# Rows of the normalised activations 2080 bytes apart instead of 2048, in one feed-forward and one convolution

## The chip, the cores and the metric

The kernel runs on one core of a Trainium2 chip, as one program. The metric is the device time of one execution in microseconds. A profile shows five engines: TensorE (PE for matmuls, PEld for loading the stationary operand), VectorE (DVE), ScalarE (ACT), GpSimd (POOL) and SyncE (SP), which issues the DMAs.

## The reference

A decoder trunk of two layers over 256 tokens of width 2048, all in float32. Layer 0 mixes tokens by multi-scale retention, layer 1 by a short gated convolution; each mixer is followed by a SwiGLU feed-forward of width 5632. Cut to the stages that the change touches:

```
h = rms_norm(x, norm2_g[0]) * (1 + sc2) + sh2          # layer 0's feed-forward
a, b = split(h @ ffn_w_in[0], 2);  x = x + g2 * ((silu(a) * b) @ ffn_w_out[0])

h = rms_norm(x, norm1_g[1]) * (1 + sc1) + sh1          # layer 1's convolution
b_gate, c_gate, u = split(h @ conv_w_in, 3)
u = c_gate * u;  y = sum(conv_w[j] * shifted(u, j) for j in range(3))
x = x + g1 * ((b_gate * y) @ conv_w_out)
```

The modulation (sc, sh, g) comes from the conditioning vector c through w_mod.

## The kernel before

**Numbers in two parts.** The width of 2048 is cut into 16 blocks of 128, one block to the 128 partitions. A float32 operand is used as two parts in a shorter format (float32r): high, the rounded value, and low, the rest. A product is then three partial products: high x high, high x low and low x high. Weights arrive by DMA as 1 MB tiles named raw; ScalarE casts 1024 columns to the high part, tile hi (L420), VectorE subtracts to get the low part, tile lo (L423). hi and lo are two fixed rings of five places of 1024 columns, and a cast waits until TensorE has read what stood in its place.

**h.** The normalised and modulated activations are one tile, h_all, of 17 x 514 columns in a partition. It holds, at different times, two layouts:

- raw rows: 16 rows, 514 columns apart: two end columns (the shift, high and low), 256 columns of scaled x (high), 256 columns (low). L642 and L643 write the 512 as x becomes ready, L654 and L655 the end columns of all rows. The first group of matmuls of a stage (L668 to L670) reads them while the norm is still being computed.
- rows of h: 16 rows of 512 columns, 256 high and 256 low. L611 (ScalarE) writes the high half, L612 (VectorE) the low half, each in the place of raw rows that have been read.

```
P, S, KT, ENDS, EARLIER = 128, 256, 16, 2, 120
h_all = hpool.tile([P, (KT + 1) * (ENDS + 2 * S)], F32R, tag="h", name="h")
```

In the retention and both feed-forwards the rows of h begin at column EARLIER of h_all, in the convolution at column 0.

**Two forms of product.** In the form by columns (`product`) the weights are stationary and h streams past: for each row k and block of 128 columns, one matmul with hi and 512 columns of h (L473), one with lo and h's 256 high columns (L476). All of the convolution's input and the first groups of each feed-forward have this form. In the form by token (`by_token`, `thrice`) 128 tokens of a row of h are stationary and 512 columns of hi or lo stream past, three matmuls for one product:

```
nc.tensor.matmul(o, hi, w_hi, start=first, stop=False)    # L486: high part of h, tile hi
nc.tensor.matmul(o, hi, w_lo, start=False, stop=False)    # L487: high part of h, tile lo
nc.tensor.matmul(o, lo, w_hi, start=False, stop=last)     # L488: low part of h, tile hi
```

Every matmul is preceded by its own load of the stationary operand (LDWEIGHTS), which runs while the matmul before it streams.

**The feed-forward's input.** It is made in column groups of 2 x 512. Each group runs over eight pairs of rows of h. Five are plain: for each of the two rows two column halves, two token halves and three matmuls, 12 per row. The other three (pairs 2, 4 and 6) use a scheme with seven products instead of eight (`sevens`), of which each is again a triple L486 to L488; the stationary operands are, in this order, s4, a12, s1, s3, a11, s2, a22. Here a11, s3 stand in the even row of the pair (s3 has replaced a part of it), a12 and a22 in the odd row, and s1, s2, s4 are sums of them in tiles of their own. Layer 0's feed-forward has four groups in its first part and six in its second. The same scheme serves in the last feed-forward's output, where mid takes h's place and the sums lie in in_cb, sums_of_tokens and other tiles.

**Order.** TensorE's order is the order in which the code is written; the other engines' is set by a scheduler, which weighs when an operand is ready. Pads such as `beside_in_sums` or `aside` hold no data; they set where the tiles behind them begin.

Of the kernel before, what the change touches and what calls it, by code (L numbers as in the profile page):

```python
# [19 lines left out]
S = 256  # L20
KT = D // P
# [22 lines left out]
ONE_GROUP = (1, 1)  # L44
FFN_TILES, FFN_SEVEN, FFN_TURNS = (20, 24), (2, 4, 6), 2
STORE_AT, LOAD_AT = 0, 2
BESIDE_IN_SUMS = 120
LEAD_RET, LEAD_CONV, LEAD_FFN = 6, 4, 2
AHEAD = 2
MOD_LEAD = 64  # L50
# [7 lines left out]
LEFT, ENDS, EARLIER = 8, 2, 120  # L58
# [207 lines left out]
def trunk(ctx: ExitStack, tc: tile.TileContext, x_in, c_in, pos_in, w_mod, cols_in, gain_in, tab_in, w_all, out):  # L266
# [12 lines left out]
    def tmp(tag, shape=(P, S), dtype=F32, pool=work, bufs=None):  # L279
        return pool.tile(list(shape), dtype, tag=tag, name=name(tag), bufs=bufs)  # L280
# [12 lines left out]
    at = [0]  # L293
# [332 lines left out]
    h_all = hpool.tile([P, (KT + 1) * (ENDS + 2 * S)], F32R, tag="h", name="h")  # L626
    hpool.tile([P, 88], F32, tag="beside", name="beside")

    def rows_at(o):
        return [  # L630
            h_all[:, o + 2 * S * j : o + 2 * S * (j + 1)].rearrange("p (a b) -> p a b", a=2) for j in range(KT)
        ]

    h = rows_at(EARLIER)
    raw_all = h_all.rearrange("p (k n) -> p k n", k=KT + 1)[:, :KT, :]

    def scaled_only(layer, norm, j):

        needed(layer, SC2 if norm else SC1, j)
        a = mod_a[layer][norm][:, j : j + 1]  # L640
        high, low = raw_all[:, j, ENDS : ENDS + S], raw_all[:, j, ENDS + S :]
        nc.scalar.activation(high, x[j], AF.Identity, scale=a)  # L642
        nc.vector.scalar_tensor_tensor(low, x[j], a, high.bitcast(F32), op0=ALU.mult, op1=ALU.subtract)  # L643
# [50 lines left out]
    def output(groups, act, which, last, after=None, base=None):  # L694

        layer, gate = which[0], mod_g[which[0]][which[1] == GT2]
        first, *groups = groups
        base, acc = first.ks[0] if base is None else base, None
        held_ks = first.ks[8 :: len(first.ks)]
        banks = product(  # L700
            first, act, base, last=False, before=lambda k: waiting.pop(0)() if waiting and k in held_ks else None
        )
        for j, g in enumerate(groups):
            needed(*which, j)
            col = gate[:, j : j + 1]
            if last and j == KT - 1:
                (pt,) = packed(g, act, base)
                nc.vector.scalar_tensor_tensor(x[j], pt[:, 0, :], col, x[j], op0=ALU.mult, op1=ALU.add)
                acc = [acc, squares(None, x[j], "acc1")]
                if after:  # L710
                    after(j)
                return acc
            (pt,) = product(g, act, base, banks=banks[j : j + 1])
            t = tmp("sum", bufs=4)
            nc.vector.scalar_tensor_tensor(t, pt[:, 1, :], col, x[j], op0=ALU.mult, op1=ALU.add)
            nc.vector.scalar_tensor_tensor(x[j], pt[:, 0, :], col, t, op0=ALU.mult, op1=ALU.add)
            if last:
                acc = squares(acc, x[j])
            if after:
                after(j)  # L720


    with ExitStack() as inner:
# [64 lines left out]
        with tc.tile_pool(name="start", bufs=1) as sp:  # L788
# [169 lines left out]
            at, plain_rows = 0.0, range(PLAIN - FIRST_KS)  # L958
# [186 lines left out]
        for n, head in enumerate(HEAD_ORDER):  # L1145
            projections(head)
            if n == HEADS // 2 - 1:
                ret_out(0, False)
        acc = ret_out(1, True)
        h = rows_at(0)  # L1150

    def sums(g):
# [38 lines left out]
    def made_in_sums(rows, single_sums):  # L1191

        for i in rows:
            both = half_bank().rearrange("p (a b) -> p a b", a=2)
            for n in range(2):
                k = 2 * i + n
                high, low = [h[k].bitcast(F32)[:, v, :] for v in range(2)]
                nc.vector.tensor_tensor(both[:, n, :], high, low, op=ALU.add)
            own["sums"][i] = [single_sums.pop() for _ in range(3)]
            tokens_sums_of(*parts(both), h[2 * i][:, :, P:], own["sums"][i])  # L1200
# [72 lines left out]
    def last_input(groups, pairs, seven):  # L1273

        ours, extra = gathered(groups, h, 0, own["sums"])
        for (t, j), pt in ours.items():
            nc.vector.tensor_tensor(extra[t, j], pt, extra[t, j], op=ALU.add)
        ms = []
        for t in range(2):
            m = extra[t, 0]  # L1280
            nc.scalar.activation(m, m, AF.Silu)
            nc.vector.tensor_tensor(m, m, extra[t, 1], op=ALU.mult)
            ms.append(m)

        def turned():
            for n, (dst, of) in enumerate(zip(pairs, seven)):
                pt = bank()
                for i in range(2):
                    for t, m in enumerate(ms):
                        c = slice((2 * n + i) * P, (2 * n + i + 1) * P)  # L1290
                        nc.tensor.transpose(pt[:, i, t * P : (t + 1) * P], m[:, c], ident)  # L1291
                if of is not None:
                    both = half_bank().rearrange("p (a b) -> p a b", a=2)
                    nc.scalar.copy(both, pt)
                nc.scalar.copy(dst[:, :, 0, :], pt)
                nc.vector.tensor_tensor(dst[:, :, 1, :], pt, dst[:, :, 0, :].bitcast(F32), op=ALU.subtract)
                if of is not None:
                    tokens_sums_of(*parts(both), of[3] if len(of) > 3 else dst[:, 0, :, P:], of[:3])

        waiting.append(turned)  # L1300

    def first_rows(firsts, pairs, layer, norm, turns=()):

        pending, done = [], 0
        for i, g in enumerate(firsts):
            pending += [sums(g)] if i else normed(acc, layer, norm, g)
            while len(pending) >= 2:
                both = half_bank().rearrange("p (a b) -> p a b", a=2)
                g1, m = both[:, 0, :], both[:, 1, :]
                silu_times(*pending[:2], g1, m)  # L1310
                pending = pending[2:]
                split(pairs[done // 2][:, done % 2], m)
                done += 1
            for turn_of in turns[4 * (i - 1) : 4 * i] if i else ():
                turn_of()

    def paired(pool, n):

        return [pool.tile([P, 2, 2, S], F32R, tag=f"mid{i}", name=name("mid")) for i in range(n // 2)]

    with tc.tile_pool(name="ffn", bufs=1) as fpool:
        h = rows_at(EARLIER)
        own.update(pool=fpool, sums={}, turns=FFN_TURNS)
        first_mid = paired(fpool, max(FFN_TILES))[: FFN_TILES[0] // 2]
        differences[0] = fpool.tile([P, 2 * DV], F32, tag="differences", name="differences")
        own["extra"] = [fpool.tile([P, DV], F32, tag=f"extra{i}", name=f"extra{i}") for i in range(2)]
        for part in range(2):
            n = FFN_TILES[part] // 2
            mid = paired(fpool, FFN_TILES[part]) if part else first_mid
            if not part:  # L1330
                first_rows(FFN_FIRSTS, mid[-2:], 0, 1)
                fpool.tile([P, BESIDE_IN_SUMS], F32, tag="beside_sums", name="beside_in_sums")
                made_in_sums(FFN_SEVEN, [
                    fpool.tile([P, 2, P], F32R, tag=f"sums{i}", name=f"sums{i}") for i in range(6)
                ] + [tmp("u", (P, 2, P), F32R, bufs=3) for _ in range(3)])
            for i, groups in enumerate(FFN_IN[part]):
                last_input(groups, mid[2 * i : 2 * i + 2], [None, None])
            act = {k + part * FFN_TILES[0]: mid[k // 2][:, k % 2] for k in range(2 * n)}
            acc = output(
                FFN_OUT[part], act, (0, GT2), part == 1, (lambda j: scaled_only(1, 0, j)) if part else None, base=0  # L1340
            )
        h = rows_at(0)

    mixing = ctx.enter_context(ExitStack())
    mpool = mixing.enter_context(tc.tile_pool(name="mpool", bufs=1))
# [3 lines left out]
    for i, g in enumerate(CONV_IN):  # L1349
        pending += [sums(g)] if i else normed(acc, 1, 0, g)  # L1350
        while len(pending) >= 3:
            pb, pc, pu = pending[:3]
            pending = pending[3:]
            j = done
            b, c, u = pb(tmp("bsum", pool=mpool, bufs=2)), pc(), pu()
# [20 lines left out]
    h = rows_at(EARLIER)  # L1376
# [187 lines left out]
```

## Time and profile before

| what | value |
|---|---|
| runs | 2564.65, 2557.89, 2558.99 us; median 2558.99 |
| profiled execution | 2558.53 us, its span 2556.8 us |
| TensorE busy | 2539.5 us, 99% of the span, granted clock 0.999 |
| VectorE, ScalarE, GpSimd busy | 92%, 53%, 7% |
| read from HBM | 685.11 MB, mean 269 GB/s |

Some rows of the profile are groups: line, engine, operation, output<-inputs, shapes, count; then busy time in us and the mean ns of one; then the idle time before them. Others are the timeline: start in us from the span's start, duration in us, engine, line, operation and, in brackets, idle time before it with what ended it. TensorE's matmuls are pipelined, so a row's duration is longer than the distance to the next row's start; the pace is read from the starts, which the timeline gives to 10 ns.

### The profile page before, as it was taken

The numbers are of one execution on the slowest core, as the hardware profiler recorded it, in microseconds if no ns is written. First come the engines' busy times: TensorE is split into PE (matmuls) and PEld (weight loads), VectorE is DVE, ScalarE is ACT, GpSimd is POOL, SyncE is SP. The second block draws the span as 40 slices with busy tenths as digits, with TensorE's granted clock in tenths as the row PEclk, the third lists the DMA queues.
The fourth block names the chain that finished last, engine by engine and source line by source line (L and its number), as shares of the span: only waits on it lengthen the run. The fifth ranks groups of instructions, "written<-read, shape, count | busy, mean of one in ns | idle before, by whom it ended". The sixth has DMA issues, their size and how long they took to land.

```text
span 2556.8 us, 34847 instructions
## 1 busy us (share of the span) xinstructions
PE 2539.5 (99%) x13281; PEld 2181.8 (85%) x13281; DVE 2353.6 (92%) x2967; ACT 1353.1 (53%) x1800; POOL 181.3 (7%) x234
## 2 busy tenths in 40 slices
PE   9999999999999999999999999999999999999998
PEld 7898888888889888888888898888998888888886
DVE  7989999898899999889999899888989999999998
ACT  5544543454456555345555454445566655555555
POOL 0000121111110001000000012000000000000001
PEclk9999999999999999999999999999999999999999
DMA  9987888978875667866568879888846465555653
GB/s 399 391 335 259 320 318 334 341 281 330 333 280 215 232 234 299 335 250 229 216 230 302 323 275 342 315 309 307 323 154 216 179 230 215 183 212 183 229 183 146
DMA packets 96697, 689.49 MB, mean 270 GB/s; under 512 B 10744, under 2 KB 12168, under 8 KB 13456
## 3 DMA queue, kind: packets, MB, share of 16 engines
q1 hardware_dynamic: 96528, 687.25, 72.2%
q8 instruction: 104, 1.70, 0.3%
q14 instruction: 65, 0.53, 0.1%
HBM read 685.11 MB, written 2.11 MB: 269 GB/s over the span
## 4 chain that ended last, share of the span: by engine, by line
PE 94%; DVE 3%; DMA 2%; ACT 1%; issue 1%; SPq 0%; POOL 0%; ACTq 0%; POOLq 0%; DVEq 0%
PE bank L473 22%; PE bank L486 17%; PE bank L487 17%; PE bank L488 17%; PE bank L476 11%; DVE lo L423 1%; PE bank L668 1%; PE bank L670 1%; PE bank L669 1%; PE bank L537 1%; PE bank L536 1%; PE bank L535 1%; DVE raw L799 1%; PE bank L1291 1%; DMA raw<-w_all 1%; PE bank L1068 1%
## 5 line engine op out<-in xcount | busy, mean ns | idle before, releaser
L420 ACT CAST hi<-raw 128x1024 fp32r<-128x1024 f32 (+1 forms) x984 | 991.6, 1019 | 927.2 <-PE bank L488 324.5
L423 DVE TENSOR_TENSOR lo<-raw,hi 128x1024 fp32r<-128x1024 f32 (+1 forms) x984 | 1141.2, 1176 | 118.7 <-ACT hi L420 110.4
L486 PE MATMUL bank<-hi,h 128*128 128x512 f32 x1540 | 601.6, 391 | 0.0
L487 PE MATMUL bank<-lo,h 128*128 128x512 f32 x1540 | 600.0, 390 | 0.0
L488 PE MATMUL bank<-hi,h 128*128 128x512 f32 x1540 | 599.6, 389 | 0.0
L327 DVE SCALAR_TENSOR_TENSOR raw<-raw,cb 128x2048 f32<-128x2048 f32 x160 | 365.1, 2283 | 12.8 <-DMA raw<-w_mod 12.6
L473 PE MATMUL bank<-h,hi 128*128 128x512 f32 x1012 | 352.8, 392 | 0.0
L488 PEld LDWEIGHTS bank<-hi,h 128*128 128x128 f32 x1540 | 289.1, 188 | 60.8
L486 PEld LDWEIGHTS bank<-hi,h 128*128 128x128 f32 x1540 | 289.3, 188 | 57.9
L487 PEld LDWEIGHTS bank<-lo,h 128*128 128x128 f32 x1540 | 289.4, 188 | 57.2
L473 PE MATMUL bank<-mid,hi 128*128 128x512 f32 x920 | 319.4, 390 | 0.0
L476 PE MATMUL bank<-h,lo 128*128 128x256 f32 x1012 | 284.7, 281 | 0.0
L476 PE MATMUL bank<-mid,lo 128*128 128x256 f32 x920 | 259.4, 282 | 0.0
L473 PEld LDWEIGHTS bank<-h,hi 128*128 128x128 f32 x1012 | 189.9, 188 | 40.9
L473 PEld LDWEIGHTS bank<-mid,hi 128*128 128x128 f32 x920 | 172.7, 188 | 36.2
L476 PEld LDWEIGHTS bank<-h,lo 128*128 128x128 f32 x1012 | 191.2, 189 | 0.5
L476 PEld LDWEIGHTS bank<-mid,lo 128*128 128x128 f32 x920 | 173.9, 189 | 0.1
L473 PE MATMUL bank<-rm,hi 128*128 128x512 f32 x496 | 172.5, 390 | 0.0
L476 PE MATMUL bank<-rm,lo 128*128 128x256 f32 x496 | 139.8, 282 | 0.0
L486 PE MATMUL bank<-hi,mid 128*128 128x512 f32 x284 | 110.8, 390 | 0.0
L488 PE MATMUL bank<-hi,mid 128*128 128x512 f32 x284 | 110.7, 390 | 0.0
L487 PE MATMUL bank<-lo,mid 128*128 128x512 f32 x284 | 110.6, 389 | 0.0
(301 smaller groups left out, 3343.7 us busy)
## 6 DMA issues: line engine op xcount, KB each, us to landing
raw<-w_all SPq DMA_DIRECT2D x456, 1024.0 KB, 4.9
raw<-w_mod SPq DMA_DIRECT2D x192, 1024.0 KB, 5.7
x<-x_in SPq DMA_DIRECT2D x4, 512.0 KB, 5.4
out<-xt SPq DMA_DIRECT2D x4, 512.0 KB, 2.7
decay<-tab_in SPq DMA_DIRECT2D x8, 128.0 KB, 5.0
x<-gate_row SPq DMA_DIRECT2D x2, 512.0 KB, 4.5
last_gain<-gain_in SPq DMA_DIRECT2D x1, 1024.0 KB
cols<-cols_in SPq DMA_DIRECT2D x1, 152.0 KB, 7.8
```

The source lines that it names most:

```text
L327: nc.vector.scalar_tensor_tensor(raw, raw, 1.0, cb, op0=ALU.mult, op1=ALU.mult, accum_out=total)
L420: nc.scalar.copy(hi[:, o], raw[:, o])
L423: nc.vector.tensor_tensor(lo, raw, hi.bitcast(F32), op=ALU.subtract)
L473: nc.tensor.matmul(pt, hi, h, start=fresh and k == g.ks[0], stop=False, skip_group_check=True)
L476: nc.tensor.matmul(pt[:, 1, :], lo, h[:, 0, :], start=False, stop=last and k == g.ks[-1], skip_group_check=True)
L486: nc.tensor.matmul(o, hi, w_hi, start=first, stop=False)
L487: nc.tensor.matmul(o, hi, w_lo, start=False, stop=False)
L488: nc.tensor.matmul(o, lo, w_hi, start=False, stop=last)
L535: nc.tensor.matmul(pt, hi, h[:, 0, :], start=first, stop=False, skip_group_check=True)
L536: nc.tensor.matmul(pt, hi, h[:, 1, :], start=False, stop=False, skip_group_check=True)
L537: nc.tensor.matmul(pt, lo, h[:, 0, :], start=False, stop=last, skip_group_check=True)
L668: nc.tensor.matmul(pt, hi, high, start=k == 0, stop=False, skip_group_check=True)
```

## The change

`rows_at` takes a second argument, a number of columns left free behind each row. Layer 0's feed-forward and the convolution pass 8, which is 32 bytes; the retention and layer 1's feed-forward pass none. Row j of h then begins 32 j bytes further on than before, while hi and lo stay where they are. No tile moves or grows: row 15 ends at column 120 + 15 x 520 + 512 = 8432 of 8738.

```
-BESIDE_IN_SUMS = 120
+BESIDE_IN_SUMS, APART = 120, 8
...
-    def rows_at(o):
-        return [
-            h_all[:, o + 2 * S * j : o + 2 * S * (j + 1)].rearrange("p (a b) -> p a b", a=2) for j in range(KT)
-        ]
+    def rows_at(o, apart=0):
+        at = [o + (2 * S + apart) * j for j in range(KT)]
+        return [h_all[:, i : i + 2 * S].rearrange("p (a b) -> p a b", a=2) for i in at]
...
     with tc.tile_pool(name="ffn", bufs=1) as fpool:
-        h = rows_at(EARLIER)
+        h = rows_at(EARLIER, APART)
...
-        h = rows_at(0)
+        h = rows_at(0, APART)
```

The order of TensorE, GpSimd and SyncE stays as it was, and so does VectorE's. On ScalarE the cast of the end columns (L654, L653 in the changed code, which is a line shorter there) moves at two places. The first is the end of layer 0's feed-forward input; s_87 is the shift of the convolution, and the numbers count tiles. Before:

```order
763 L420 CAST hi<-raw_11132 128x1024
764 L420 CAST hi<-raw_11154 128x1024 x2
765 L654 CAST h<-s_87 128x16
766 L420 CAST hi<-raw_11199 128x1024
767 L1281 ACTIVATE extra_6715<-extra_6715 128x512
```

And now:

```order
763 L420 CAST hi<-raw_11132 128x1024
764 L420 CAST hi<-raw_11154 128x1024
765 L653 CAST h<-s_87 128x16
766 L420 CAST hi<-raw_11154 128x1024
767 L420 CAST hi<-raw_11199 128x1024
768 L1280 ACTIVATE extra_6715<-extra_6715 128x512
```

The small cast has moved ahead of the second half of raw_11154. The second place, on ScalarE too, is the end of the convolution's input; s_88 is the shift of layer 1's feed-forward. Before:

```order
1031 L420 CAST hi<-raw_14982 128x1024
1032 L545 COPY low_14964<-bank_14912 128x256
1033 L654 CAST h<-s_88 128x16
1034 L420 CAST hi<-raw_14982 128x1024
1035 L1360 ACTIVATE y_14971<-cu_14968,cols 128x256
```

And now:

```order
1031 L420 CAST hi<-raw_14913 128x1024
1032 L653 CAST h<-s_88 128x16
1033 L420 CAST hi<-raw_14982 128x1024
1034 L545 COPY low_14964<-bank_14912 128x256
1035 L420 CAST hi<-raw_14982 128x1024
1036 L1359 ACTIVATE y_14971<-cu_14968,cols 128x256
```

Here it has moved ahead of the first half of raw_14982 and of a copy. At both places it now waits for TensorE itself.

## The prediction

> **What bounds the kernel now.** I read the page first: engine shares, granted clock and the chain that ended last, then the costliest groups.
>
> ```profile
> PE 2539.5 (99%) x13281; PEld 2181.8 (85%) x13281; DVE 2353.6 (92%) x2967; ACT 1353.1 (53%) x1800; POOL 181.3 (7%) x234
> PEclk9999999999999999999999999999999999999999
> PE 94%; DVE 3%; DMA 2%; ACT 1%; issue 1%; SPq 0%; POOL 0%; ACTq 0%; POOLq 0%; DVEq 0%
> L486 PE MATMUL bank<-hi,h 128*128 128x512 f32 x1540 | 601.6, 391 | 0.0
> L473 PE MATMUL bank<-h,hi 128*128 128x512 f32 x1012 | 352.8, 392 | 0.0
> L476 PE MATMUL bank<-h,lo 128*128 128x256 f32 x1012 | 284.7, 281 | 0.0
> ```
>
> TensorE is busy for 99% of the span at its full clock, it carries 94% of the chain, and the matmuls that use h waited for nothing (0.0). So the time is the sum of the distances from one matmul's start to the next, and a change of addresses can only count there. The duration of a row (389 to 392 ns) does not help, since neighbours overlap; I therefore went to the timeline of PE and took differences of start times.
>
> The first look is at by-token matmuls in the changed feed-forward, where a 128x128 block of h is loaded as weights and 512 columns of hi or lo stream past. One group of eight row pairs holds 5x24 + 3x21 = 183 of them in a row; its second and its last:
>
> ```profile
> 872.58 0.40 PE L487 MATMUL bank<-lo,u 128*128 128x512 f32 x1
> ...
> 913.65 0.39 PE L488 MATMUL bank<-hi,h 128*128 128x512 f32 x1
> ```
>
> 181 steps in 41.07 us are 226.9 ns each. Call 226.7 ns the settled pace (21 steps in 4.76 us, below).
>
> The second look asks whether addresses matter at all. In the built program hi and lo begin at bytes 43,616 and 64,096 of a partition, both 32 past a multiple of 64, and h at 117,376, a multiple of 64. EARLIER adds 480 bytes, so all rows of h in the feed-forward now stand at 32 past a multiple of 64, like the weights: I call that equal, and 32 bytes off it odd. One tile of the last feed-forward is odd: in_cb, in cb's place at byte 1,152. It is loaded as weights in three triples (L486, L487, L488) of a seven, a block of 21 matmuls. Another seven takes sums_of_tokens, which is equal, instead:
>
> ```profile
> 2085.51 0.40 PE L488 MATMUL bank<-hi,mid 128*128 128x512 f32 x1
> 2085.75 0.39 PE L486 MATMUL bank<-hi,in_cb 128*128 128x512 f32 x1
> 2085.98 0.39 PE L487 MATMUL bank<-lo,in_cb 128*128 128x512 f32 x1
> 2086.21 0.39 PE L488 MATMUL bank<-hi,in_cb 128*128 128x512 f32 x1
> 2086.44 0.40 PE L486 MATMUL bank<-hi,mid 128*128 128x512 f32 x1
> ...
> 2090.61 0.39 PE L486 MATMUL bank<-hi,mid 128*128 128x512 f32 x1
> ...
> 2091.30 0.39 PE L486 MATMUL bank<-hi,mid 128*128 128x512 f32 x1
> ...
> 2096.06 0.39 PE L486 MATMUL bank<-hi,sums_of_tokens 128*128 128x512 f32 x1
> ...
> 2100.82 0.39 PE L486 MATMUL bank<-hi,mid 128*128 128x512 f32 x1
> ```
>
> With sums_of_tokens 21 steps take 4.76 us. With in_cb the 25 steps from 2085.51 (one before the seven) to 2091.30 (three after it, where the pace is back) take 5.79 us; at 226.7 ns they would take 5.67. The seven's three odd triples cost 0.123 us, 41 ns each. Of that the step into the triple is 240 ns instead of 227, its three steps are 230 each (0.69 us), and the remaining 20 ns or so fall on the equal matmuls behind it. So what costs is to change from equal to odd and back, and perhaps a slower pace while odd.
>
> **The change part by part.** No instruction is added or removed. Row j of h moves to 32 j bytes further on, so rows 0, 2, .. 14 keep their relation to the weights and rows 1, 3, .. 15 lose it, in both stages.
>
> *By-token matmuls of layer 0's feed-forward.* There are 10 groups. In each, five normal row pairs have one odd row of 12 matmuls in a row: 50 blocks of 12. In each seven, order s4, a12, s1, s3, a11, s2, a22, the triples a12 and a22 come from the odd row: 30 sevens, 60 single triples. A single triple is priced directly: 60 x 41 ns = 2.5 us. A block of 12 costs 41 ns if the pace recovers within it, and 41 + 9 x 3.3 = 71 ns if the odd pace of 230 lasts; the three odd steps show no recovery, so I lean to the second and take 64: 50 x 64 ns = 3.2 us. Bounds: 110 x 41 ns = 4.5 us below; above, if nothing settles any more, 0.123 us / 25 = 4.9 ns on each of 1830 matmuls, 9.0 us.
>
> *The convolution's input.* Here weights are hi and lo, and h streams, 512 columns and then 256: a pair per row. Before, with no offset, all rows are odd; after, the even-numbered ones stay odd and the others become equal. Both states occur already: equal in the feed-forward's first groups (48 pairs from 802.42 to 819.07), odd in the convolution (688 pairs from 1517.19 to 1755.70), and equal again in the retention, two columns at a time (24 pairs from 548.13 to 556.62, and a later batch):
>
> ```profile
> 548.13 0.39 PE L473 MATMUL bank<-h,hi 128*128 128x512 f32 x1
> ...
> 556.62 0.38 PE L1088 MATMUL bank<-tab,o 128*128 128x128 f32 x2
> ...
> 559.92 0.40 PE L473 MATMUL bank<-h,hi 128*128 128x512 f32 x1
> ...
> 560.27 0.39 PE L473 MATMUL bank<-h,hi 128*128 128x512 f32 x1
> ...
> 560.61 0.40 PE L473 MATMUL bank<-h,hi 128*128 128x512 f32 x1
> ...
> 802.42 0.39 PE L473 MATMUL bank<-h,hi 128*128 128x512 f32 x1
> ...
> 819.07 0.39 PE L486 MATMUL bank<-hi,h 128*128 128x512 f32 x1
> ...
> 1517.19 0.39 PE L473 MATMUL bank<-h,hi 128*128 128x512 f32 x1
> ...
> 1755.70 0.39 PE L473 MATMUL bank<-mid,hi 128*128 128x512 f32 x1
> ```
>
> Equal: 16.65 us / 48 = 346.9 ns. Odd: 238.51 / 688 = 346.7 ns. When settled, neither is better, so only the alternation can cost. The retention's batch never settles: 8.49 / 24 = 353.7 ns. The later one has pairs of 350 and 340 in turn, 0.69 us for two, the settled mean. Nothing in this trace alternates row by row with these two matmuls. Bounds for 688 pairs: all at 353.7, +4.8 us; half of them at 340 to 343 and half settled, about -1.5 us. The nearest row is the entry into a settled state: the 48 equal pairs include one, and come out 0.01 us above 48 x 346.7. That bounds a change of state at 10 ns; the later batch says a disturbed pace can average to nothing. I take 1.5 ns for each of 688 changes: +1.0 us. The feed-forward's 48 pairs at the same price: +0.1 us.
>
> *What else moves.* Three things, all priced at nothing. h's new rows in the convolution reach into the next raw row, so the VectorE writes of h (L612) now wait until TensorE has read one raw row more. The order also puts the small ScalarE cast L654 one or two places earlier, where it waits for TensorE itself.
>
> ```profile
> 1349.46 0.39 PE L488 MATMUL bank<-hi,h 128*128 128x512 f32 x1
> 1350.57 1.05 ACT L420 CAST hi<-raw 128x1024 fp32r<-128x1024 f32 x1 [1.28 <-PE bank L488]
> 1351.52 0.22 ACT L654 CAST h<-s 128x16 fp32r<-128x16 f32 x1
> 1515.42 0.28 PE L668 MATMUL bank<-h,hi 128*128 128x258 f32 x1
> 1516.97 0.86 DVE L612 SCALAR_TENSOR_TENSOR h<-u,s,h 128x256 fp32r<-128x256 f32 x2
> 1755.00 0.39 PE L473 MATMUL bank<-h,hi 128*128 128x512 f32 x1
> 1755.82 1.06 ACT L420 CAST hi<-raw 128x1024 fp32r<-128x1024 f32 x1 [1.76 <-PE bank L473]
> 1757.04 0.22 ACT L654 CAST h<-s 128x16 fp32r<-128x16 f32 x1
> ```
>
> L612 writes rows 12 and 13 from 1516.97; row 13 now needs raw row 14, and the first matmul of raw row 15 (L668) had begun at 1515.42, 1.5 us earlier. The cast in the feed-forward writes one column of each raw row, the last of which now lies in row 14's first half of low values; its last reader starts at 1349.46 and ends by 1349.85. It then runs 0.22 us in the 1.28 us in which ScalarE stood idle, ahead of the cast to hi at 1350.57, which waits for TensorE anyway. In the convolution the last reader is the row-14 matmul at 1755.00, over by 1755.39, and 0.22 us more is still ahead of 1755.82. If that cover were gone, each would cost at most its 0.22 us once. VectorE (92%) gets no longer instruction, and a slower TensorE gives it slack. SP's and POOL's queues are unchanged.
>
> **Sum.** 2.5 + 3.2 + 1.0 + 0.1 = 6.8 us on the profiled execution's 2558.53 us (span 2556.8): 2565.3 us. That execution stands 0.46 us below the runs' median of 2558.99; I don't shift the forecast for it. Against the median it is +0.25%. About 0.3%, 7.7 us, is what a measurement of this kernel can tell from no change, so the forecast lies just inside "no change".
>
> **Rivals.**
>
> *Addresses do nothing, so the change does not do what its distance suggests.* Then two streams into TensorE never meet, and the time stays at 2558.5 us. For it: both settled paces of the pairs are 346.7 ns, whatever the offset. Against it: in_cb's 41 ns per triple, though that tile differs from sums_of_tokens in more than its offset (it lies elsewhere, in cb's place). Chance 0.10; this is the rival on the other side, not slower, and it decides if the odd by-token matmuls stay at 226.7 ns. The Trainium skill stands behind it: "SBUF — State Buffer", section "SBUF: two separate sides", says that on the engine side only the port pair shared by VectorE and GpSimd contends and that TensorE waits for no one, and "TensorE: Matmul & The Clock Gate", section "Step-by-step: what each phase is for", gives TensorE one read port for the streamed operand and another for the weights. By these the sum is 0; the trace disagrees as far as in_cb's rows go.
>
> *The convolution never settles.* Each row comes in at the wrong moment for the next, as in the retention's batch at 353.7 ns. Then 688 x 7.0 = 4.8 us there instead of 1.0, and with 5.8 us in the feed-forward 2569.1 us. For it: every row changes state, which no stage does now. Against it: entries into settled states are cheap. Chance 0.20.
>
> *Gain.* Pairs alternate 340 and 350 at present in one batch; if the odd step let every second pair keep the short one, -1.5 us in the convolution, and by-token blocks that recover at once would leave +4.5, or with rival one's mechanism 0: 2557 to 2561.5 us. Chance 0.05, and under -0.3% only if the by-token pace fell below 226.7, which no row shows.
>
> *The moved cast or the longer waits hold ScalarE or VectorE up.* Each would then delay hi or lo by up to 0.22 us at one place, or a few times that: 2566 us. Chance 0.03.
>
> **How the numbers follow.** The likeliest case has 0.62 and its own range, 4.5 to 6.5 us by token and 0 to 2.5 in the pairs: 2563.0 to 2567.6; about a quarter of it (0.16) lies past 2566.7, where slower by 0.3% begins. Slower: 0.16 + 0.20 + 0.01 = 0.37. Within: 0.46 + 0.10 + 0.03 + 0.02 = 0.61. Faster: 0.02. For 8 in 10 the range leaves out no effect and the gain below (0.13) and the worst of the unsettled convolution above: 2561.0 to 2569.8.
>
> **What would show it.** In the changed kernel's timeline of PE: a group's 183 by-token matmuls take some 0.55 us more (5 x 64 + 6 x 41 ns = 0.57), with steps of about 230 ns in odd rows and 235 at their edges; L486 to L488 in layer 1's feed-forward keep their pace. The 688 pairs of the convolution take 238.5 to 241 us. The last feed-forward and the retention keep their lengths to 0.1 us. The prediction is wrong if odd blocks keep 226.7 ns (then 2558.5), if the pairs take over 242 us, or if a new wait stands before L473, L476 or L486.

## The result, and the profile after

The changed kernel takes 2569.54 us in the median (2569.48 to 2569.63, 5 runs), the kernel before 2558.99 us (2557.89 to 2564.65, 5 runs). The ratio is 1.0042 with a 95% interval of 1.0032 to 1.0053: 10.55 us slower, 0.41%. The forecast was 2565.3 us with a range of 2561.0 to 2569.8: the sign and the range hold, the range by 0.3 us at its upper end, the size is short by 4.2 us, and "within 0.3%", which had most of the chance, did not come; "slower" did.

The page of the changed kernel, with engine shares, granted clock by slices, the chain that ended last and the groups that use h:

```profile
PE 2553.0 (99%) x13281; PEld 2181.8 (85%) x13281; DVE 2354.8 (92%) x2967; ACT 1352.6 (53%) x1800; POOL 180.4 (7%) x234
PEclk9999999999999999999999999999999999999999
PE 93%; DVE 4%; DMA 1%; issue 1%; ACT 1%; POOL 0%; ACTq 0%; POOLq 0%; SPq 0%; DVEq 0%
L486 PE MATMUL bank<-hi,h 128*128 128x512 f32 x1540 | 604.0, 392 | 0.0
L473 PE MATMUL bank<-h,hi 128*128 128x512 f32 x1012 | 355.9, 395 | 0.0
L476 PE MATMUL bank<-h,lo 128*128 128x256 f32 x1012 | 283.3, 280 | 0.0
```

Counts, clock and the zero idle time are as before. TensorE's busy time grew by 13.5 us, the span from 2556.8 to 2567.8, and no wait has come in: the same matmuls start further apart. Weight loads (PEld) take the same 2181.8 us in all.

The timeline of TensorE, changed kernel (start in us, duration, line, operands). The rows are the first of layer 0's first pairs, the first by-token matmul behind them, the second and the last of the group of 183, the first pair of the convolution's 688 and the first matmul behind those:

```profile
802.01 0.39 PE L473 MATMUL bank<-h,hi 128*128 128x512 f32 x1
...
818.84 0.40 PE L486 MATMUL bank<-hi,h 128*128 128x512 f32 x1
...
873.52 0.39 PE L487 MATMUL bank<-lo,u 128*128 128x512 f32 x1
...
915.47 0.40 PE L488 MATMUL bank<-hi,h 128*128 128x512 f32 x1
...
1526.04 0.39 PE L473 MATMUL bank<-h,hi 128*128 128x512 f32 x1
...
1767.41 0.40 PE L473 MATMUL bank<-mid,hi 128*128 128x512 f32 x1
```

The 181 steps of the group take 41.95 us instead of 41.07 (+0.88, forecast 0.55). The 688 pairs take 241.37 us instead of 238.51 (+2.86, forecast 1.0). The first 48 pairs take 16.83 instead of 16.65 (+0.2, forecast 0.1). Summed over all 1830 by-token matmuls of layer 0's feed-forward, from the differences of starts in ns, the by-token matmuls take 9.2 us more (forecast 5.7). The changed stages so come to +12.2 us; some 1.1 us go the other way at the two ends of the execution (0.4 in the first 70 us, 0.7 behind the last matmul), where no address changed, and leave the 11.0 us by which the spans differ. The kernel with 256 bytes below, whose stages are unchanged, is 0.7 us shorter behind the last matmul too, four of the other kernels are shorter there by the same 0.7 us and the rest by 0.2 at most, and most others are 0.1 to 0.4 us shorter in the first 70 us; I take the 1.1 us for chance in the profiled executions, which no run here proves.

What the next rows show is the key to the miss. They are from the same group: row 6 of h from 878.17, row 7 from 880.93, and, from 886.03 to 887.39, six matmuls of which the first five take row 8:

```profile
878.17 0.40 PE L486 MATMUL bank<-hi,h 128*128 128x512 f32 x1
...
880.93 0.40 PE L486 MATMUL bank<-hi,h 128*128 128x512 f32 x1
...
883.73 0.39 PE L486 MATMUL bank<-hi,sums 128*128 128x512 f32 x1
...
886.03 0.39 PE L487 MATMUL bank<-lo,h 128*128 128x512 f32 x1
...
887.39 0.39 PE L487 MATMUL bank<-lo,sums 128*128 128x512 f32 x1
```

Row 7, 12 steps in 2.80 us, runs at 233.3 ns. Row 6, which the forecast called equal, takes 2.76 us, 230.0 ns. Only at row 8 is the settled pace there: 1.36 us / 6 = 226.7 ns. Row 6 lies 192 bytes from where it was, row 8 lies 256 bytes from it. So "equal" was the wrong class.

### The profile page after: what moved, and what is told of

It reads as the page before. It is cut to its first block, busy times and chain, and to the rows that moved or that the text cites. A ratio compares the mean times of both kernels' runs of the same rounds, so it can differ in the third digit from the quotient of the medians.

```text
span 2567.8 us, 34855 instructions
## 1 busy us (share of the span) xinstructions
PE 2553.0 (99%) x13281; PEld 2181.8 (85%) x13281; DVE 2354.8 (92%) x2967; ACT 1352.6 (53%) x1800; POOL 180.4 (7%) x234
## 4 chain that ended last, share of the span: by engine, by line
PE 93%; DVE 4%; DMA 1%; issue 1%; ACT 1%; POOL 0%; ACTq 0%; POOLq 0%; SPq 0%; DVEq 0%
PE bank L473 22%; PE bank L486 17%; PE bank L487 17%; PE bank L488 17%; PE bank L476 11%; DVE lo L423 2%; PE bank L667 1%; PE bank L669 1%; PE bank L668 1%; PE bank L537 1%; PE bank L536 1%; PE bank L535 1%; DVE raw L798 1%; DMA raw<-w_all 1%; PE bank L1290 1%
## 5 line engine op out<-in xcount | busy, mean ns | idle before, releaser
L486 PE MATMUL bank<-hi,h 128*128 128x512 f32 x1540 | 604.0, 392 | 0.0
L327 DVE SCALAR_TENSOR_TENSOR raw<-raw,cb 128x2048 f32<-128x2048 f32 x160 | 365.3, 2285 | 11.1 <-DMA raw<-w_mod 10.7
L473 PE MATMUL bank<-h,hi 128*128 128x512 f32 x1012 | 355.9, 395 | 0.0
L486 PEld LDWEIGHTS bank<-hi,h 128*128 128x128 f32 x1540 | 289.3, 188 | 60.4
L473 PE MATMUL bank<-mid,hi 128*128 128x512 f32 x920 | 319.4, 390 | 0.0
L476 PE MATMUL bank<-h,lo 128*128 128x256 f32 x1012 | 283.3, 280 | 0.0
L476 PE MATMUL bank<-mid,lo 128*128 128x256 f32 x920 | 259.4, 282 | 0.0
L473 PEld LDWEIGHTS bank<-h,hi 128*128 128x128 f32 x1012 | 190.0, 188 | 45.3
L473 PEld LDWEIGHTS bank<-mid,hi 128*128 128x128 f32 x920 | 172.7, 188 | 36.2
L476 PEld LDWEIGHTS bank<-h,lo 128*128 128x128 f32 x1012 | 190.3, 188 | 0.5
L476 PEld LDWEIGHTS bank<-mid,lo 128*128 128x128 f32 x920 | 173.9, 189 | 0.1
L473 PE MATMUL bank<-rm,hi 128*128 128x512 f32 x496 | 172.5, 390 | 0.0
L476 PE MATMUL bank<-rm,lo 128*128 128x256 f32 x496 | 139.8, 282 | 0.0
L486 PE MATMUL bank<-hi,mid 128*128 128x512 f32 x284 | 110.8, 390 | 0.0
```

The source lines that it names most:

```text
L327: nc.vector.scalar_tensor_tensor(raw, raw, 1.0, cb, op0=ALU.mult, op1=ALU.mult, accum_out=total)
L473: nc.tensor.matmul(pt, hi, h, start=fresh and k == g.ks[0], stop=False, skip_group_check=True)
L476: nc.tensor.matmul(pt[:, 1, :], lo, h[:, 0, :], start=False, stop=last and k == g.ks[-1], skip_group_check=True)
```

## The experiments

Below, "distance" is the start of h's row less the start of hi or lo, modulo 256 bytes: hi (43,616) and lo (64,096) are both at 96, h is at 96 in layer 0's feed-forward before (distance 0) and at 128 in the convolution before (distance 32). In the changed kernel row j has 32 j added. The table gives, for every kernel in which h or all the tiles moved, the change against the kernel before in the three stages, worked out from the starts of the same matmuls in the two traces (us):

| kernel | bytes added | by token, 1830 matmuls | convolution, 688 pairs | first 48 pairs |
|---|---|---|---|---|
| changed kernel | 32 j, both stages | +9.2 | +2.86 | +0.19 |
| e1_ffn_only | 32 j, feed-forward alone | +9.2 | 0.00 | +0.18 |
| e2_halves | 32 for rows 8 to 15 | +5.4 | +1.43 | +0.03 |
| e3_pairs | 32 for every second two rows | +6.6 | +1.15 | +0.15 |
| e4_64_bytes | 64 j | +6.7 | +3.43 | +0.13 |
| e5_all_one | 32 for all rows | +10.7 | +1.52 | 0.00 |
| e7_halves_64 | 64 for rows 8 to 15 | +5.5 | +2.67 | +0.18 |
| e7_halves_128 | 128 for rows 8 to 15 | +4.9 | +0.57 | +0.17 |
| e7_halves_256 | 256 for rows 8 to 15 | +0.2 | 0.00 | 0.00 |
| e9_all_moved | 32 for every tile but `ones`, hi and lo too | 0.0 | 0.00 | 0.00 |

**One stage alone.**

```
-        h = rows_at(0, APART)
+        h = rows_at(0)
```

> The offset in the feed-forward alone; the convolution's rows lie 2048 bytes apart again. If the two stages cost independently, the feed-forward's ten by-token groups keep the changed kernel's lengths (42.5 us where it was 41.6) and the convolution's 688 pairs return from 241.4 to 238.5 us: about 2.9 us less than the changed kernel, some 2566.7 us. Rival: the moved casts and longer waits cost something, then the pairs stay above 238.5.

Measured: 2566.75 us (5 runs), ratio 1.0033 [1.0020, 1.0046]. The by-token groups are as in the changed kernel. The first pair of the convolution and the first matmul behind its 688 pairs, on the timeline of TensorE:

```profile
1526.19 0.39 PE L473 MATMUL bank<-h,hi 128*128 128x512 f32 x1
...
1764.70 0.39 PE L473 MATMUL bank<-mid,hi 128*128 128x512 f32 x1
```

238.51 us, as before. So the two stages count separately, and the convolution's 2.86 us are its own.

**Fewer changes of state.**

```
-        at = [o + (2 * S + apart) * j for j in range(KT)]
+        at = [o + 2 * S * j + apart * (j // 8) for j in range(KT)]
```

> Rows 8 to 15 lie 32 bytes further on, rows 0 to 7 where they were, so a column group changes relation once between plain rows, not at every row. Theory of changes (each change from equal to odd disturbs the matmuls behind it, a settled odd matmul costs 3.3 ns): 48 plain odd matmuls at 230 ns and two sevens that mix odd rows with equal sums, 0.4 to 0.5 us per group, 4.5 to 5 us in all; convolution 238.5 to 238.8 us. Theory of odd matmuls (each odd one costs 8.9 us / 780 = 11.4 ns wherever it stands): 720 of them, 8.2 us, by-token groups at 42.4 us.

Measured: 2565.07 us (one run), by token +5.4, convolution +1.43. That is above the 4.5 to 5 us and the 0 to 0.3 us of the theory of changes, and by token far below the 8.2 us of the other. The kernel with every second two rows moved (below) makes more changes between the same two distances:

```
-        at = [o + (2 * S + apart) * j for j in range(KT)]
+        at = [o + 2 * S * j + apart * (j // 2 % 2) for j in range(KT)]
```

> Rows 2, 3, 6, 7, 10, 11, 14 and 15 lie 32 bytes further on, so the relation changes after every second row, 24 matmuls, and the sevens use equal rows alone. Theory of changes, with recovery inside 24 matmuls: each odd block 24 x 3.3 ns and some 28 ns at its edges, 4 per group, 0.43 us per group, 4.3 us in all; without recovery some 5 ns on each of 1830 matmuls, 9 us. Theory of odd matmuls: 960 x 11.4 ns = 10.9 us. The convolution has half as many changes: by the first theory half of its 2.9 us.

Its rows overlap by 8 columns where a moved one is followed by an unmoved one, so there it computes with other values. Measured: 2565.15 us (one run), by token +6.6, convolution +1.15; none of the three sums expected by token came. So by token the number of changes is not what costs: sorted by distance, the normal row pairs' matmuls at 32 stand 6.7 ns above the pace of before in the first of the two (478 matmuls, +3.20 us) and 6.4 ns in the second (950 matmuls, +6.11 us); those at distance 0 stand 0.2 and 0.4 ns above it. The pace while odd is the price there. In halves, what the forecast assumed comes true: the unmoved rows are back at 226.7 ns in some ten matmuls.

**All rows moved by the same 32 bytes**, so that nothing alternates between rows:

```
-        h = rows_at(EARLIER, APART)
+        h = rows_at(EARLIER + APART)
...
-        h = rows_at(0, APART)
+        h = rows_at(APART)
```

with the pitch of before.

> All rows lie 2048 bytes apart, and all begin 32 bytes further on: odd throughout in the feed-forward, equal throughout in the convolution. Theory of changes: plain rows settle at the odd pace of 230 ns (120 x 3.3 = 0.40 us per group) or at 226.7; the sevens mix odd rows with equal sums, 0.36 us per group; 3.6 to 7.6 us in all; the convolution keeps 238.5 us. Theory of odd matmuls: 1560 x 11.4 ns = 17.8 us, groups at 43.4 us.

Measured: 2570.55 us (one run), as slow as the changed kernel. The timeline of TensorE: the second and the last matmul of the group of 183, with seven steps from within it, and the two ends of the convolution's pairs:

```profile
874.06 0.39 PE L487 MATMUL bank<-lo,u 128*128 128x512 f32 x1
...
905.22 0.40 PE L486 MATMUL bank<-hi,h 128*128 128x512 f32 x1
905.45 0.40 PE L487 MATMUL bank<-lo,h 128*128 128x512 f32 x1
905.68 0.40 PE L488 MATMUL bank<-hi,h 128*128 128x512 f32 x1
905.91 0.40 PE L486 MATMUL bank<-hi,h 128*128 128x512 f32 x1
906.15 0.40 PE L487 MATMUL bank<-lo,h 128*128 128x512 f32 x1
906.38 0.40 PE L488 MATMUL bank<-hi,h 128*128 128x512 f32 x1
906.62 0.40 PE L486 MATMUL bank<-hi,h 128*128 128x512 f32 x1
...
916.18 0.39 PE L488 MATMUL bank<-hi,h 128*128 128x512 f32 x1
...
1527.86 0.39 PE L473 MATMUL bank<-h,hi 128*128 128x512 f32 x1
...
1767.89 0.39 PE L473 MATMUL bank<-mid,hi 128*128 128x512 f32 x1
```

The group takes 42.12 us, +1.05 against 41.07, with no alternation of rows at all: the starts settle at 235 and 231 or 232 ns in turn, 233.4 on average. And the convolution's pairs, now all at distance 64, settle at 348.9 ns: 240.03 us for 688. A distance has a pace of its own. Neither theory's sum came (+10.7 us by token, where 3.6 to 7.6 and 17.8 had been expected), and the convolution, which was to keep its 238.5 us, did not.

A rival is that h now meets the accesses of another engine. The same trace speaks against it. By the starts in ns, two steps at a time and in rows 10, 11, 14 and 15 of all ten groups, a step takes 233.2 ns where ScalarE is busy for less than a tenth of the time (114 pairs of steps) and 233.35 where it is busy for more than nine tenths (70). For VectorE it is 233.3 in both cases, though only 4 pairs find it idle, against 215. That leaves TensorE's own two operands.

**Twice the pitch's surplus**, 64 bytes from row to row instead of 32:

```
-BESIDE_IN_SUMS, APART = 120, 8
+BESIDE_IN_SUMS, APART = 120, 16
```

> Rows lie 2112 bytes apart, 64 bytes more than before instead of 32, so all of them keep their relation modulo 64. Theories of changes and of odd matmuls: no cost, groups at 41.6 us, convolution 238.5 us, time 2559 us. Rival that the uneven distance itself, the new waits or the moved casts cost: 2569 us as with 32 bytes.

Measured: 2567.82 us, ratio 1.0036 [1.0022, 1.0050]. The timeline of TensorE, the two ends of the group and of the pairs:

```profile
873.47 0.40 PE L487 MATMUL bank<-lo,u 128*128 128x512 f32 x1
...
915.18 0.40 PE L488 MATMUL bank<-hi,h 128*128 128x512 f32 x1
...
1523.77 0.39 PE L473 MATMUL bank<-h,hi 128*128 128x512 f32 x1
...
1765.70 0.40 PE L473 MATMUL bank<-mid,hi 128*128 128x512 f32 x1
```

41.71 us (+0.64) and 241.93 us (+3.42). Both theories had expected nothing, mine with the rest: modulo 64 bytes nothing had moved. In the trace the convolution's sequence of steps repeats every four rows, which are 256 bytes of surplus. That made the next theory: the distance counts modulo 256, or a larger power of two.

**in_cb moved by 32 bytes.** If 64 bytes were the period, the tile that gave the forecast its price would be equal with cb 32 bytes further on, and the sevens that take it would cost nothing more. In the kernel before:

```
-... BESIDE_CB, BESIDE_SUMS = (3, 4, 6), ((2, 4, 6, 5, 1), (2, 4, 6, 10, 8)), 2, 40, 48
+... BESIDE_CB, BESIDE_SUMS = (3, 4, 6), ((2, 4, 6, 5, 1), (2, 4, 6, 10, 8)), 2, 32, 48
...
+    const.tile([P, 8], F32, tag="ahead_of_cb", name="ahead_of_cb")
     cb = const.tile([P, D], F32, tag="cb", name="cb")
```

> The kernel before, with cb (and in_cb, which takes its place) 32 bytes further on, so that in_cb stands equal to the weights; everything else stays in its place. If in_cb's price is one of its offset, its eight sevens in the last feed-forward lose 0.12 us each, 1.0 us in all, and each of 21 matmuls takes 4.76 us. If it is one of the tile's place or of the work around it, nothing changes. On the clock 1.0 us is 0.04% and hard to see.

Measured: 2558.54 us, ratio 1.0003 [0.9993, 1.0013]. The 25 steps of the forecast's seven, on the timeline of TensorE:

```profile
2084.91 0.39 PE L489 MATMUL bank<-hi,mid 128*128 128x512 f32 x1
...
2090.68 0.39 PE L487 MATMUL bank<-hi,mid 128*128 128x512 f32 x1
```

5.77 us, against 5.79 before and 5.67 at the settled pace. The 0.12 us that each seven was to lose did not come: moving by 32 took almost nothing away, so modulo 64 falls here too. Modulo 256 it went from 32 to 64.

**The period.** Halves again, with three larger shifts, `apart * (j // 8)` with APART = 16, 32 and 64 columns:

> Rows 8 to 15 of h lie 64 bytes further on in layer 0's feed-forward and the convolution; rows 0 to 7 stay. With 32 bytes in the same place the ten groups of 183 by-token matmuls grew by 0.55 us each and the convolution's 688 pairs by 1.43 us. Theory A (only the offset modulo 64 bytes counts): 0 in both, as with the kernel before. Theory B (it counts modulo 256 or more): groups +0.3 to +0.8 us each, since the plain pairs then load an equal row and one 64 bytes off in turn, pairs +1 to +3 us.

> The same with 128 bytes for rows 8 to 15. Theory A (modulo 64): 0. Theory C (modulo 128): 0. Theory B (modulo 256 or more): groups +0.3 us or more each, or another sum than 0 in the pairs.

> The same with 256 bytes for rows 8 to 15. Theories A, B (modulo 256) and C: 0 by token and in the pairs, to 0.1 us. Theory D (no period up to 512 bytes, only that rows differ in distance): groups +0.3 us or more each.

Measured: 2567.51, 2562.96 and 2558.08 us (one run each; the first has a stop of 0.8 us ahead of the convolution that has nothing to do with h). The timeline of TensorE, the ends of the group of 183 with 64, 128 and 256 bytes, the last with the convolution's ends:

```profile
873.23 0.40 PE L487 MATMUL bank<-lo,u 128*128 128x512 f32 x1
...
914.85 0.39 PE L488 MATMUL bank<-hi,h 128*128 128x512 f32 x1
```

```profile
872.85 0.40 PE L487 MATMUL bank<-lo,u 128*128 128x512 f32 x1
...
914.41 0.39 PE L488 MATMUL bank<-hi,h 128*128 128x512 f32 x1
```

```profile
872.77 0.40 PE L487 MATMUL bank<-lo,u 128*128 128x512 f32 x1
...
913.84 0.39 PE L488 MATMUL bank<-hi,h 128*128 128x512 f32 x1
...
1517.60 0.39 PE L473 MATMUL bank<-h,hi 128*128 128x512 f32 x1
...
1756.11 0.39 PE L473 MATMUL bank<-mid,hi 128*128 128x512 f32 x1
```

41.62, 41.56 and 41.07 us; the last is what the kernel before takes, and the pairs take its 238.51 too. With 256 bytes all that is left is 0.2 us at two late steps in one group and the few behind them. So the period is 256 bytes: 64 and 128 cost, 256 does not.

**The distance or the place?** In the kernel before, a pad of 8 columns ahead of all tiles but `ones`:

```
+    const.tile([P, 8], F32, tag="ahead_of_cb", name="ahead_of_cb")
     cb = const.tile([P, D], F32, tag="cb", name="cb")
```

> The kernel before with an 8-column pad ahead of every tile, so that hi, lo, h, mid, sums and all the rest begin 32 bytes further on in the partition and keep their distances from each other; h keeps its pitch of 2048 bytes. Theory B (the distance between the two operands, modulo 256, counts): each stage keeps its length to 0.1 us, groups of 183 at 41.6 us, the convolution's pairs at 238.5 us, the whole at 2558 us. Theory E (each operand's own place modulo 256 counts, whatever the other's): hi and lo go from 96 to 128 and h from 96 to 128, so all by-token groups change, by up to the +1.05 us each of the kernel in which h alone went to 128, and the pairs with them.

Measured: 2558.14 us (one run), every stage that uses h within about 0.1 us. The ends of the group on the timeline of TensorE:

```profile
872.35 0.40 PE L488 MATMUL bank<-lo,u 128*128 128x512 f32 x1
...
913.41 0.39 PE L489 MATMUL bank<-hi,h 128*128 128x512 f32 x1
```

41.06 us with hi, lo and h all at 128 instead of 96: the distance counts, not the place, as far as one shift by 32 bytes can show it.

**The forecast's price taken away.** cb at byte 1376, which is 96 modulo 256, with all that lies behind it 256 bytes further on. As the pad above, with 56 columns, and BESIDE_CB 48:

> The kernel before with cb and all that lies behind it moved so that cb begins at byte 1376, which is 96 modulo 256 as hi, lo, mid and h are in the feed-forwards; the other tiles move by 256 bytes and keep their relations. Moved by 32 bytes, cb's sevens in the last feed-forward kept their extra 0.12 us each. Theory B (modulo 256): each of the sevens that take in_cb comes down from 4.88 to 4.76 us, the whole by 0.12 us for each such seven, about 1 us in all. Theory D or a cause in that tile's place: no change in these sevens.

Measured: 2558.01 us (11 runs) against 2558.44 (15 runs), ratio 0.9998 [0.9989, 1.0007]. The same 25 steps as above, on the timeline of TensorE:

```profile
2085.66 0.39 PE L489 MATMUL bank<-hi,mid 128*128 128x512 f32 x1
2085.88 0.39 PE L487 MATMUL bank<-hi,in_cb 128*128 128x512 f32 x1
...
2091.32 0.39 PE L487 MATMUL bank<-hi,mid 128*128 128x512 f32 x1
```

5.66 us: the 0.12 us are gone, and by the starts in ns the step into the triple is 226 instead of 235. Over the 22 steps from just before their first triple of in_cb, five of the eight sevens lose 0.12 us and the others 0.01 to 0.06, 0.68 us together, where about 1 us had been expected. Of those three, two begin right behind other, smaller matmuls, where the steps are irregular in both kernels, and one has a single late step of 278 ns. The 0.68 us are 0.03% of the whole, which its time cannot confirm; it is the one version here in which a stage of h, mid or in_cb became shorter than before by more than 0.1 us.

## Why the prediction was right where it was, and wrong where it was not

**TensorE's starts carry it all: right.** The three stages sum to the whole difference but for the ends, no wait came in ahead of L473, L476 or L486, and the clock stayed. The last feed-forward, whose addresses did not change, takes the same 25 steps in the same 5.79 us, on the timeline of the changed kernel:

```profile
2097.19 0.40 PE L488 MATMUL bank<-hi,mid 128*128 128x512 f32 x1
2097.43 0.39 PE L486 MATMUL bank<-hi,in_cb 128*128 128x512 f32 x1
...
2102.98 0.39 PE L486 MATMUL bank<-hi,mid 128*128 128x512 f32 x1
```

**The moved casts and the longer waits cost nothing: right.** ScalarE's timeline at the end of the convolution's pairs:

```profile
1764.68 1.05 ACT L420 CAST hi<-raw 128x1024 fp32r<-128x1024 f32 x1 [1.44 <-PE bank L473]
1767.19 0.22 ACT L653 CAST h<-s 128x16 fp32r<-128x16 f32 x1 [1.46 <-PE bank L473]
1767.53 1.06 ACT L420 CAST hi<-raw 128x1024 fp32r<-128x1024 f32 x1
```

The small cast waited for TensorE and was over at 1767.41, when the first matmul behind the pairs started. The cast to hi began 0.12 us after that start, as it did before (1755.82 after 1755.70). Between the last by-token matmul of layer 0's feed-forward and the convolution's pairs TensorE's starts move 0.05 us earlier against those of before, so the first place cost nothing either.

**"Equal" and "odd" modulo 64 bytes: wrong, and this is the step that failed.** The forecast put half of the rows into a class that stays at 226.7 ns. The period is 256 (64 and 128 bytes cost, 256 do not), so of the sixteen rows of the changed kernel only rows 0 and 8 stay equal, and fourteen lose it. By distance, the matmuls of the normal row pairs in the changed kernel stand above their pace of before by 5.9 ns at 32 (120 matmuls), 6.6 at 64 (240), 6.7 at 96 (232), 3.3 at 192 (240), 6.2 at 224 (238) and 0.7 at 0 (120). The even rows at 64 and 192 alone bring 2.4 us to which the forecast gave nothing, and those at 128 in the sevens 0.8 more. The trace of before held only distances 0 and 32 in by-token matmuls, so it could not tell 64 from 256; the text chose 64 without a row for it and never said that it had chosen.

**The price of an odd matmul: right in kind, too low in size.** "Perhaps a slower pace while odd" was the true part of the price, "what costs is to change" the lesser. The step into the triple, read as 240 ns from rows shown to 10 ns, is 235 by the starts in ns, and the 22 steps from there average 231.9, with the equal matmuls between the triples as slow as the odd ones: the seven had one slower pace, not three edges. The three odd steps of in_cb's triples gave 230 ns; a long odd stretch settles at 233.4, so a block of 12 costs 80 ns (12 x 6.7), not 64. The by-token sum of 5.7 us would have been good for a kernel with half of its rows at distance 32: two such kernels measured 5.4 and 6.6. What came, 9.2, lies just above the upper bound of 9.0 us, "if nothing settles any more".

**The convolution: wrong reason, mid-sized miss.** "When settled, neither is better, so only the alternation can cost" rested on two distances, 0 and 32, both 346.7 ns. A third, 64, settles at 348.9 without any alternation. In the changed kernel the rows take 346.7 ns at 160 and 224, 348.3 at 128, 350 at 0, 351 at 32 and 64, 354.2 at 96, 359.2 at 192. So 2.86 us, not 1.0 and not the rival's 4.8. The alternation does cost too: the rows at 0 and 32, whose settled pace is 346.7, bring 0.6 of the 2.86 us, and in e2_halves 344 pairs at 348.9 would make 0.8 us where 1.43 came. No run has all rows at one of the other distances, so how the rest divides between pace and change stays open. Nor is the distance all that sets the pace of such pairs: the retention's batch, at distance 0, kept 353.7 ns in the forecast's own rows.

**The rivals.** "Addresses do nothing" is out by e4, e5 and e7. The Trainium skill, "SBUF — State Buffer", section "SBUF: two separate sides", says that on the engine side only the port pair shared by VectorE and GpSimd contends and that TensorE never waits on anyone. It speaks of engines that wait for each other, and the sum of 0 that the forecast drew from it does not hold: here one and the same stream of matmuls goes from 226.7 to 233.4 ns by the distance of its two operands alone. "Gain" has nothing: no distance ran by-token matmuls below 226.7 on average. What in the chip has the period of 256 bytes, and why pairs run at full pace at distance 32 and by-token matmuls do not, no run here shows; that stays open.

**The range and the class.** The range held by luck. By token 9.2 us came where the likeliest case had 4.5 to 6.5, and 2.86 in the pairs where it had at most 2.5; the sum lies inside only because the range had room for the unsettled convolution, which did not come, and because the two ends took 1.1 us less. 12.2 us in the stages less 1.1 at the ends crosses the bound of 7.7 us, which the forecast missed by 0.9. With the even rows counted as unequal at the forecast's own prices (90 blocks at 64 ns and 100 triples at 41 ns, 9.9 us, and 1.1 us of pairs) it would have come to 11.0 us and lain on the other side.

## What to carry to other kernels

Where TensorE is the bound and both its operands come from memory on the chip, look up where the stationary and the streamed operand begin in the partition and keep their distance a multiple of 256 bytes for by-token matmuls like these; a pad of 32, 64 or 128 bytes is not free there, while one of 256 cost no more than 0.2 us. A price read from one pair of addresses says nothing about the period: before calling two placements equal, name the row that shows it, or keep the other classes in the range. A small change of pace is best read from distances of starts over a long run of the same matmuls, since 3% a step hardly shows in durations (a mean of 391 ns before and 392 after for L486).

## What the runs showed of the hardware that was not expected

- The pace of by-token matmuls (128x128 stationary, 512 columns streamed, a weight load for each) depends on the distance of the two operands modulo 256 bytes: 226.7 ns at 0, 233.4 at 32, about 233 at 64, about 232 at 128.
- The distance counts, not the place: with hi, lo and h all 32 bytes further on, no stage that uses h changed by more than about 0.1 us.
- Pairs of 512 and 256 columns with one tile's weights settle at 346.7 ns at distances 0 and 32 and at 348.9 at 64: distance 32 costs them nothing, and by-token matmuls 6.7 ns. The two forms differ in which operand is stationary and in the lengths streamed; no run tells which of these it is.
- At distance 0 a disturbance dies out: behind an interruption the steps of a by-token group go between 224 and 236 ns for some nine matmuls and then stay at 226 or 227 (kernel before). At distance 32 they stay in a short repeating pattern, 235 and 231 or 232 in turn, to the end of the group (all rows moved).
